# Gated DeltaNet's inverse: the third series of a join writes to the PSUM bank of the scan's state products

## The chip, the cores and the metric

The kernel runs on one core of one Trainium2 chip. The time is the device time of one execution in microseconds, from the chip's own clock. The profile is one execution taken with the hardware profiler. The engines are TensorE (PE in the profile; PEld is its loading of weights), VectorE (DVE), ScalarE (ACT), GpSimd (POOL) and SyncE (SP), whose queue issues most of the DMAs.

## The reference

Four layers of a decoder trunk on one sequence of 1024 positions, width 1024, all in float32: HGRN2, sliding-window attention, Gated DeltaNet, and HGRN2 again. Each layer normalises x, applies its mixer to it, gates the result and adds it back to x. The layer that the change touches is the third. Cut to its core, for one chunk of 64 positions of one of 16 heads:

```python
A = jnp.einsum('bhid,bhjd->bhij', kb, k_) * dec * strict
rhs = jnp.concatenate([v_ * beta_[..., None], kb * jnp.exp(d)[..., None]], axis=-1)
X = lax.linalg.triangular_solve(A + eye, rhs, left_side=True, lower=True, unit_diagonal=True)
u, w = X[..., :dv], X[..., dv:]
v_new = u - jnp.einsum('bhid,bhde->bhie', w, S)
o = jnp.einsum('bhid,bhde->bhie', q_ * jnp.exp(d)[..., None], S) + jnp.einsum('bhij,bhje->bhie', qk, v_new)
S = S * jnp.exp(d_last)[..., None] + jnp.einsum('bhid,bhie->bhde', k_ * jnp.exp(d_last - d)[..., None], v_new)
```

q, k and v come from an input projection, a causal convolution of four taps and a SiLU; q and k are normalised to unit length. The output is normalised, multiplied by a gate path z (SiLU) and projected back.

## The kernel before, in words

The kernel works with chunks of 128 positions. It forms the inverse of the triangular matrix (A plus the identity) outright and then multiplies with it. Two of the 16 heads share one q and k, so the layer runs in eight units (u = 0 to 7) of two heads. Three streams of work belong to a unit:

- The projections (proj_kq, proj_v, proj_z). One projection in proj_fm is 24 matmuls (eight blocks of the width, three products each, since the operands are split into a high and a low part) into one PSUM bank, for one half of the 1024 positions. Its evacuation follows: for q, k and v the convolution (conv: two copies on ScalarE, L692 and L696, three steps on VectorE, L698, a tanh, L704, and a last product, L705), then a transpose on TensorE (L711) and sums of squares on ScalarE (sumsq, L718); for z a tanh and a product (L789, L790). When both halves of q and k are through, the factors of the norms follow (L752 to L764), gd_gn among them.
- The inverse. kk_ps and qk_ps (L809, L810) are the products of k with k and with q for one half; they are evacuated with the decay and with gd_gn (L820, L824). The diagonal blocks of 32 by 32 go through DRAM into another layout and are inverted there by a forward substitution of 31 steps on VectorE (L845, L846, in gd_Tb). Then the blocks are joined to 128 by 128 in four series of small matmuls, for 16 matrices at once (two heads, eight chunks). The first (L874) and the second (L882 to L884) join 32 to 64 and write two tiles each, the third (L891) and the fourth (L899) join 64 to 128 and write one each. ScalarE and VectorE copy the results out between them: L885 copies the second series' result into gd_Z, which the third reads; L886 and L887 copy other parts of it into gd_uq; L895 and L896 copy the third's result into gd_Z for the fourth; L901 and L902 store the fourth's.
- The scan (scan). It goes through eight chunks in order with the state S: ks_ps (L942, L943), w_ps (L953, L969) and, in seven chunks of eight, S_ps (L958), which VectorE adds to the decayed state (L962, L964).

weave calls the streams in turn, by their shares of the work done so far, and so sets the order in which the code's instructions are written: first inverse(0) with projections of units 0 to 2, then scan(u) with inverse(u+1), projections and the adaLN product of the next layer. A scheduler at build time then orders each engine's queue: among the instructions that can go, those with the higher priority first, and otherwise those that were written first. The inverse's series have the highest priority (burst); tied keeps each series together.

PSUM has eight banks, handed out under tags by psum: "proj" has two, "lev" two (kk_ps, qk_ps and the tiles z_ps of the series), "ta", "tr", "o" and "s" one each. A tile holds its bank until its last reader is done. S_ps uses "ta". So do the projections in part: proj_ps counts its calls modulo self.pb and gives one call of pb = 3 to "ta". pb is 3 in most of the kernel, 2 in the weaves that have a scan of Gated DeltaNet (then no projection takes "ta"), and still 3 in the first weave:

```python
self.np_ = (self.np_ + 1) % self.pb
return self.psum("ta" if self.np_ == 2 else "proj", name, 1 if self.np_ == 2 else 2)
```

Buffers in SBUF have tags of the same kind; conv, sumsq and z's evacuation share "tb" with four.

Of the kernel before, what the change touches and what calls it, by code (L numbers as in the profile page):

```python
# [81 lines left out]
class Trunk:  # L82
# [501 lines left out]
    def gdn(self, i, side):  # L584
# [210 lines left out]
        def inverse(u, dd):  # L795
# [46 lines left out]
            for j in range(31):  # L842
                n, m = 31 - j, j // 2 + 1
# [22 lines left out]
            bank = lambda name, m: self.psum("lev", name, 2).rearrange("p (g m) -> p g m", m=m)  # L866
# [20 lines left out]
            nc.vector.tensor_copy(uv[R[0], :, R[1]], za[R[0]])  # L887
            yield 1300

            z = bank("z_ps", 64)  # L890
            self.tied([lambda g=g, q=q: nc.tensor.matmul(z[q, g % 8, :], uv[lo, g, up], Z[lo, g, :], start=True, stop=True)  # L891
                       for n in range(8) for g, q in ((n, up), (n + 8, lo))])
            for b in (0, 1):
# [4 lines left out]
            z = bank("z_ps", 64)  # L898
# [29 lines left out]
        def scan(u, dd):  # L928
# [3 lines left out]
            for n in range(C):  # L932
# [53 lines left out]
        decays()  # L986
        drain(proj_kq(0, ds[0], ((1,),)))
        weave(self.tc, (inverse(0, ds[0]), 28000, 0, 0.8, 100),
              (chain(proj_z(0, ds[0], (1,)), proj_v(0, ds[0]), proj_z(1, ds[1], (1,)), proj_kq(1, ds[1])), 62400, 0, 1, 0))
        self.pb = 2  # L990
        for u in range(U):
            cs = [proj_z(x, ds[x], hv) for x, *hv in ZL[u]]
            tot = 10400 * sum(len(z) - 1 for z in ZL[u])
            if u + 2 < U:
                cs.append(proj_kq(u + 2, ds[u + 2]))
                tot += 20800
            if u + 1 < U:
                cs.append(proj_v(u + 1, ds[u + 1]))
                tot += 20800
            st_ = [(scan(u, ds[u]), 18000, 0, 1, PR[0])]  # L1000
            if u + 1 < U:
                st_.append((inverse(u + 1, ds[u + 1]), 28000, 0, 1, PR[1]))
            else:
                self.fill_x(0)
                cs += [self.out_load(od, 0, KT, 0, gp, "tmp", 2, (self.zd, "tb", bufs["tb"])), self.out_mm(i, w_out, 0, KT, 0, on), self.out_load(od, 0, KT, 1, gp, "tmp", 2, (self.zd, "tb", bufs["tb"]))]
                tot += 41600
            weave(self.tc, *st_, (chain(*cs), tot, 0, 1, 0), (take(side, NS[2]), NS[2], 0, 1, 0))
# [644 lines left out]
```

## Time and profile before

| | |
|---|---|
| median of 3 runs | 2649.19 us (2645.78 to 2649.27) |
| profiled execution | 2648.82 us, span 2647.1 us |
| busy: TensorE, VectorE, ScalarE, GpSimd | 97%, 76%, 50%, 6% of the span |
| granted TensorE clock, mean over the span | 0.992 |
| Gated DeltaNet's inverses | the third series' first matmul at 1242.7 us, its last at 1859.8 us |
| DMA | 308.91 MB, 117 GB/s |

Times in the profile count from the span's start. A row of the timeline gives start, length, engine, line, operation and tiles, and in brackets how long the engine stood idle before it and what released it. A row of the windows gives, for each engine in turn, the busy time and the number of instructions, then the granted TensorE clock, the DMA share and GB/s. In a line's own view the pairs behind "its engine sat idle before it" are us in total and times.

### The profile page before, as it was taken

To read this page: it belongs to the slowest core of one execution; us is meant where nothing else is said; L and a number is where in the kernel's file an instruction comes from. 1 tells how busy PE (TensorE), PEld (TensorE's weight loads), DVE (VectorE), ACT (ScalarE), POOL (GpSimd) and SP (SyncE) were. 2 spreads that over 40 slices of the span, in tenths; PEclk is the share of its full clock that TensorE was granted. 3 is DMA by queue.
4 is the path that set the end of the run, shared out by engine and by line. 5 is a ranking of instruction groups with operands and counts; after the bars stand their busy time and mean duration, and the time that the engine had idled before them with its cause. 6 is when DMAs were issued, how large, how long until landed. Compare 5 with 4: busy or idle time off the path is not lost.

```text
span 2647.1 us, 50764 instructions
## 1 busy us (share of the span) xinstructions
PE 2560.9 (97%) x18271; PEld 2041.4 (77%) x18271; DVE 2016.7 (76%) x5651; ACT 1322.4 (50%) x3466; POOL 161.4 (6%) x382
## 2 busy tenths in 40 slices
PE   7999999999999999999999999999899999999998
PEld 4777777688878867777777777778678877787777
DVE  5485788777787878768899989988776837368675
ACT  3343444443464655545666666666544434245452
POOL 0001000011000000101000100110221000000010
PEclk8999999999999999999999999999999999999999
DMA  7333343544233252534444344333585312122343
GB/s 260 95 114 97 108 142 115 166 138 132 67 101 101 73 165 90 149 94 117 105 110 108 102 119 112 93 88 101 175 247 171 116 49 80 40 82 65 123 140 116
DMA packets 387281, 308.91 MB, mean 117 GB/s; under 512 B 74787, under 2 KB 313814, under 8 KB 387030
## 3 DMA queue, kind: packets, MB, share of 16 engines
q1 hardware_dynamic: 374486, 264.77, 34.4%
q0 software_dynamic: 12544, 40.90, 4.9%
q8 instruction: 144, 2.36, 0.4%
q14 instruction: 107, 0.88, 0.1%
HBM read 244.70 MB, written 60.88 MB: 115 GB/s over the span
## 4 chain that ended last, share of the span: by engine, by line
PE 74%; DVE 12%; DMA 5%; ACT 4%; issue 3%; SPq 0%; POOL 0%; DVEq 0%; POOLq 0%; ACTq 0%
PE proj_ps L222 10%; PE proj_ps L224 10%; PE proj_ps L223 10%; PE outp_ps L222 5%; PE outp_ps L223 5%; PE outp_ps L224 4%; PE projw_ps L223 2%; PE projw_ps L222 2%; PE projw_ps L224 2%; DVE gd_tb L698 1%; PE projt_ps L223 1%; PE projt_ps L224 1%; PE projt_ps L222 1%; DVE w_lo L194 1%; PE w_ps L953 1%
## 5 line engine op out<-in xcount | busy, mean ns | idle before, releaser
L222 PE MATMUL proj_ps<-hhi,w_hi 128*128 128x512 f32 x1664 | 676.7, 407 | 3.6 <-ACT gd_tb L696 3.3
L223 PE MATMUL proj_ps<-hlo,w_hi 128*128 128x512 f32 x1664 | 672.7, 404 | 0.0
L224 PE MATMUL proj_ps<-hhi,w_lo 128*128 128x512 f32 x1664 | 672.1, 404 | 0.0
L222 PEld LDWEIGHTS proj_ps<-hhi,w_hi 128*128 128x128 f32 x1664 | 315.0, 189 | 64.6 <-ACT gd_tb L696 5.9
L224 PEld LDWEIGHTS proj_ps<-hhi,w_lo 128*128 128x128 f32 x1664 | 314.7, 189 | 58.1 <-issue 0.4
L223 PEld LDWEIGHTS proj_ps<-hlo,w_hi 128*128 128x128 f32 x1664 | 315.2, 189 | 55.2 <-issue 0.9
L194 DVE TENSOR_TENSOR w_lo<-w_raw,w_hi 128x512 fp32r<-128x512 f32 x344 | 231.4, 677 | 142.3 <-ACT w_hi L193 139.6
L193 ACT CAST w_hi<-w_raw 128x512 fp32r<-128x512 f32 x344 | 209.5, 612 | 260.6 <-PE proj_ps L223 151.3
L222 PE MATMUL outp_ps<-o_hi,w_hi 128*128 128x512 f32 x576 | 230.2, 402 | 9.2 <-ACT o_hi L1323 7.4
L223 PE MATMUL outp_ps<-o_lo,w_hi 128*128 128x512 f32 x576 | 230.3, 400 | 2.4 <-DVE o_lo L1324 2.3
L224 PE MATMUL outp_ps<-o_hi,w_lo 128*128 128x512 f32 x576 | 228.8, 398 | 0.5 <-DVE w_lo L194 0.5
L196 ACT ACTIVATE w_hi<-w_raw,par 128x512 fp32r<-128x512 f32 (+1 forms) x136 | 94.8, 697 | 131.2 <-PE outp_ps L223 93.1
L698 DVE SCALAR_TENSOR_TENSOR gd_tb<-gd_xs,taps,gd_tb 128x512 f32<-128x512 f32 x192 | 146.2, 762 | 15.9 <-ACT gd_tb L696 12.0
L222 PEld LDWEIGHTS outp_ps<-o_hi,w_hi 128*128 128x128 f32 x576 | 109.5, 190 | 33.4 <-ACT o_hi L1323 9.1
L448 DVE SCALAR_TENSOR_TENSOR ada_acc<-ada_w,par,ada_acc 128x512 f32<-128x512 f32 x154 | 115.1, 748 | 21.1 <-DMA ada_w<-in_ada_w_dram 19.9
L223 PEld LDWEIGHTS outp_ps<-o_lo,w_hi 128*128 128x128 f32 x576 | 109.7, 190 | 26.3 <-DVE o_lo L1324 4.4
L197 DVE SCALAR_TENSOR_TENSOR w_lo<-w_raw,par,w_hi 128x512 fp32r<-128x512 f32 (+1 forms) x136 | 97.0, 716 | 41.4 <-ACT w_hi L196 40.7
L224 PEld LDWEIGHTS outp_ps<-o_hi,w_lo 128*128 128x128 f32 x576 | 109.5, 190 | 22.9 <-DVE w_lo L194 1.0
L1315 POOL DMA_DIRECT2D o_in<-od x72 | 38.8, 539 | 1214.9 <-DMA w_raw<-in_hg_out_w_dram 429.2
L222 PE MATMUL projw_ps<-w_hi,hhi 128*128 128x512 f32 x256 | 102.4, 405 | 2.3 <-DVE hg_q L1041 2.3
L223 PE MATMUL projw_ps<-w_lo,hhi 128*128 128x512 f32 x256 | 103.6, 406 | 0.2 <-DVE w_lo L194 0.2
L224 PE MATMUL projw_ps<-w_hi,hlo 128*128 128x512 f32 x256 | 102.2, 400 | 0.0
(429 smaller groups left out, 5365.7 us busy)
## 6 DMA issues: line engine op xcount, KB each, us to landing
ada_w<-in_ada_w_dram SPq DMA_DIRECT2D x160, 256.0 KB, 2.8
w_raw<-in_hg_in_w_dram SPq DMA_DIRECT2D x136, 256.0 KB, 2.8
w_raw<-in_gd_in_w_dram SPq DMA_DIRECT2D x128, 256.0 KB, 3.0
o_in<-od POOLq DMA_DIRECT2D x72, 256.0 KB, 3.5
x<-xd SPq DMA_DIRECT2D x64, 256.0 KB, 4.5
w_raw<-in_gd_out_w_dram SPq DMA_DIRECT2D x64, 256.0 KB, 3.2
xd<-x POOLq DMA_DIRECT2D x48, 256.0 KB, 2.7
w_raw<-in_sw_in_w_dram SPq DMA_DIRECT2D x44, 256.0 KB, 3.0
```

The lines of the kernel that those rows point to most:

```text
L193: nc.scalar.copy(hi, raw)
L194: nc.vector.tensor_tensor(lo, raw, hi.bitcast(F32), ALU.subtract)
L196: nc.scalar.activation(hi, raw, AF.Copy, scale=scale)
L197: nc.vector.scalar_tensor_tensor(lo, raw, scale, hi.bitcast(F32), ALU.mult, ALU.subtract)
L222: mm(out, a[0], b[0], start=start, stop=False)
L223: mm(out, a[0], b[1], start=False, stop=False)
L224: mm(out, a[1], b[0], start=False, stop=stop)
L448: self.step = self.nc.vector.scalar_tensor_tensor(acc, w, c, acc, ALU.mult, ALU.add)
L698: last = nc.vector.scalar_tensor_tensor(y, xs[:, j:j + HT], w(j), y, ALU.mult, ALU.add)
L953: nc.tensor.matmul(po[:, hd[a]], dd["u"][a, hf][:, cs], rhs, start=True, stop=True)
L1315: nc.gpsimd.dma_start(t, od[(k0 + k) * P:(k0 + k + 1) * P, sl])
```

## The change

One line of inverse is changed: the third series' tile is allocated under "ta", the tag of S_ps, and not under "lev". Shape, matmuls, priority and the copies behind it stay as they are. The fourth series' tile and all others stay in "lev".

```diff
             nc.vector.tensor_copy(uv[R[0], :, R[1]], za[R[0]])
             yield 1300
 
-            z = bank("z_ps", 64)
+            z = self.psum("ta", "z_ps", 1).rearrange("p (g m) -> p g m", m=64)
             self.tied([lambda g=g, q=q: nc.tensor.matmul(z[q, g % 8, :], uv[lo, g, up], Z[lo, g, :], start=True, stop=True)
                        for n in range(8) for g, q in ((n, up), (n + 8, lo))])
             for b in (0, 1):
                 nc.gpsimd.tensor_copy(uv[R[b], :, R[b]], Uc[R[b]])
             nc.scalar.copy(Z[up, 0:8], z[up])
             nc.vector.tensor_copy(Z[up, 8:16], z[lo])
```

## The prediction

> **What bounds the kernel now.** I read the page first, then the busy time by window over the Gated DeltaNet layer, then the third series' own line, then the timelines round it. The page gives the span and who fills it:
>
> ```profile
> span 2647.1 us, 50764 instructions
> PE 2560.9 (97%) x18271; PEld 2041.4 (77%) x18271; DVE 2016.7 (76%) x5651; ACT 1322.4 (50%) x3466; POOL 161.4 (6%) x382
> ...
> PE 74%; DVE 12%; DMA 5%; ACT 4%; issue 3%; SPq 0%; POOL 0%; DVEq 0%; POOLq 0%; ACTq 0%
> ```
>
> The chain of waits that ends last is 74% TensorE. The windows (length, then busy time per engine, PE first) show it for the stretch that the change touches:
>
> ```profile
> 1215.00:1250.00 35.00, 32.13 (x356) 25.96 (x357) 28.70 (x64) 21.23 (x67) 6.73 (x12) 1.00 0.48 123
> 1250.00:1870.00 620.00, 606.28 (x4415) 485.90 (x4414) 558.92 (x1625) 392.33 (x1244) 54.33 (x137) 0.99 0.41 107
> ```
>
> From 1250 to 1870 TensorE rests for 13.7 of 620 us, so a hole closed on TensorE should mostly be time, and a hole opened costs about its length. The third series is L891; its own view says what PE waited for:
>
> ```profile
> L891 PE MATMUL z_ps<-gd_Z,gd_uq x256: 218/218/312, 1242.7 to 1859.9; 64*64 64x64 f32 x128
> ...
>   DVE gd_uq L886: 7.2, 7
> ```
>
> Seven of its eight runs wait, 7.2 us in all, for VectorE's copy L886. L886 writes partitions 64 to 95 of gd_uq; the series reads partitions 0 to 63. It is no operand. L886 is the last reader of the second tile of the series before, so the wait is for that tile's bank in the ring of two. That is what the change removes.
>
> **The gain.** What then still holds the series is its operand gd_Z, copied by ScalarE at L885. The timelines of units 0, 4 and 7 (start, length in us; idle time and releaser in brackets):
>
> ```profile
> 1240.66 0.40 PE L222 MATMUL proj_ps<-hhi,w_hi 128*128 128x512 f32 x1
> 1241.64 0.58 ACT L885 COPY gd_Z<-z_ps 32x512 f32<-32x512 f32 x1
> 1242.66 1.15 PE L891 MATMUL z_ps<-gd_Z,gd_uq 64*64 64x64 f32 x32 [1.60 <-DVE gd_uq L886]
> ...
> 1600.85 0.58 ACT L885 COPY gd_Z<-z_ps 32x512 f32<-32x512 f32 x1 [0.33 <-PE z_ps L884]
> 1602.29 0.69 DVE L886 COPY gd_uq<-z_ps 32x512 f32<-32x512 f32 x1
> 1603.12 1.15 PE L891 MATMUL z_ps<-gd_Z,gd_uq 64*64 64x64 f32 x32 [1.03 <-DVE gd_uq L886]
> ...
> 1857.35 0.58 ACT L885 COPY gd_Z<-z_ps 32x512 f32<-32x512 f32 x1 [0.54 <-PE z_ps L884]
> 1858.97 1.15 PE L891 MATMUL z_ps<-gd_Z,gd_uq 64*64 64x64 f32 x32 [0.40 <-DVE gd_uq L886]
> ```
>
> In units 4 and 7 ScalarE is through (1601.43, 1857.93) before PE runs out of projection (1603.12 - 1.03 = 1602.09, 1858.57), and the whole hole goes. In unit 0 ScalarE ends at 1242.22, and some 0.3 of the 1.6 us could go. Units 1 to 7 hold 7.2 - 1.6 = 5.6 us. The matmuls and the two copies of the result (L895, L896) are the same in any bank. A wait can come back behind the hole, as VectorE keeps its queue: the fourth series of unit 0 stands 0.47 us for L896. So 5.6 is the most, 0 the least, and I take 85%: **-4.7 us**.
>
> **The new bank.** It is tag "ta", one buffer. In units 1 to 7 only the scan's S_ps (L958) uses it. In the code's order the series of unit u+1 stands after all seven S_ps of scan u and before those of scan u+1, which need this inverse's result:
>
> ```profile
> L958 PE MATMUL S_ps<-gd_ws,gd_kt x112: 377/379/483, 1250.4 to 1929.6; 128*128 128x256 f32 x112
> ```
>
> Unit 0's first S_ps starts at 1250.4, 4.2 us behind the series' last reader (L896, below, until 1246.16). No wait there: 0. In "lev" the fourth series and the next unit's kk_ps now find a bank earlier, but both wait for more than that (L896; the fourth series): 0 too.
>
> In the first weave it is otherwise. There proj_ps counts modulo three, and every third projection takes "ta". Counted through the code, 198 calls have been made when inverse(0) allocates the third series' tile; calls 199 and 200 follow, and 200 = 3*66 + 2 is the one that takes "ta". It is q of unit 1, second half. **In the code's order it stands behind the series; in time it ran long before it:**
>
> ```profile
> 1222.09 0.57 ACT L692 COPY gd_xs<-proj_ps 128x512 f32<-128x512 f32 x1
> 1228.37 0.58 ACT L692 COPY gd_xs<-proj_ps 128x512 f32<-128x512 f32 x1
> 1231.01 0.28 ACT L718 ACTIVATE gd_tb<-qtr_ps 128x128 f32<-128x128 f32 x1 [1.47 <-PE qtr_ps L711]
> 1232.03 0.71 ACT L696 ACTIVATE gd_tb<-proj_ps,taps 128x512 f32<-128x512 f32 x1
> 1238.17 0.93 DVE L705 SCALAR_TENSOR_TENSOR gd_q<-gd_tb 128x512 f32<-128x512 f32 x1
> 1243.24 0.28 ACT L718 ACTIVATE gd_tb<-qtr_ps 128x128 f32<-128x128 f32 x1
> 1245.01 0.60 ACT L789 ACTIVATE gd_tb<-proj_ps 128x512 f32<-128x512 f32 x1
> 1245.48 0.68 DVE L896 COPY gd_Z<-z_ps 64x512 f32<-64x512 f32 x1
> 1246.29 0.68 DVE L790 SCALAR_TENSOR_TENSOR gd_tb<-gd_tb,proj_ps 128x512 f32<-128x512 f32 x1
> 1248.53 0.48 PE L222 MATMUL proj_ps<-hhi,w_hi 128*128 128x512 f32 x1
> ```
>
> (The two L692, with L696, are the evacuations of q's halves; L718 their sums of squares; L789 and L790 evacuate the z projection behind them, and the last row starts the next one that then has a bank.) So it matters whether buffers of one tag are given out in the code's order or to whoever is ready. Two places speak for the code's order. The first is the ring of two:
>
> ```profile
> 1222.27 0.69 DVE L705 SCALAR_TENSOR_TENSOR gd_k<-gd_tb 128x512 f32<-128x512 f32 x1
> 1242.55 0.68 DVE L887 COPY gd_uq<-z_ps 32x512 f32<-32x512 f32 x1
> 1246.31 1.15 PE L899 MATMUL z_ps<-gd_uq,gd_Z 64*64 64x64 f32 x32 [0.47 <-DVE gd_Z L896]
> 1247.39 1.16 PE L809 MATMUL kk_ps<-gd_k 128*128 128x128 f32 x8
> ```
>
> After L887 (1243.23) one bank of "lev" is empty. Unit 1's kk_ps has had its k since 1222.96, yet starts only right behind the fourth series, which the code allocates first. The second is L789: the z projection's evacuation needs a buffer of tag "tb" and comes right behind the L718 of q's second half, whose buffer of that tag stands before it in the code. I take it that the order is the code's. Then call 200 waits for L896 of unit 0.
>
> **What that costs.** The projection leaves 1222 and starts behind L896. With its own VectorE work (L698, L705) and ScalarE work (L704, L696) gone from the inverse's way I put L896 some 3 us earlier, at 1243 (0 earlier is the other end). It is 24 matmuls; from the evacuation at 1222.09 to that at 1228.37 is 6.3 us with a transpose between, so 5.5 us alone, to 1248.5. Up to here TensorE has the z projections behind it (two banks "proj") to do in its stead, so nothing is lost yet. Then they are both full, and the next needs L790, which is queued behind the late one's evacuation. From evacuation to first L718 was 8.9 us for q's first half (1222.09 to 1231.01) and 14.9 for the second; I take 9, then L789 and L790, 1.3: the next projection starts at 1258.8 and not at 1248.5. In between TensorE has the scan; the projections' own share is:
>
> ```profile
> 1248.50:1258.00 9.50, 5.12 (x18) 3.09 (x18) 0.00 (x0) 0.00 (x0) 1.00 0.35 95
> 1278.00:1318.00 40.00, 15.42 (x62) 0.00 (x0) 1.00 0.27 73
> 1811.00:1842.00 31.00, 15.62 (x62) 0.00 (x0) 1.00 0.31 89
> 1252.85 0.17 DVE L762 TENSOR_SCALAR gd_gn<-gd_gm 128x16 f32<-128x16 f32 x1
> ```
>
> (first row: proj_ps alone; second and third: the forward substitution's gd_Tb in units 1 and 7.) 5.12/9.5 of 10.3 us is **+5.5 us**. The ends: 0, if other work fills the gap; 1246.2 + 5.5 + 14.9 + 1.3 = 1267.9, so 19.4 us late, times 0.54, +10.5.
>
> Third, the factor gd_gn, which the evacuation of unit 1's kk_ps needs, moves from 1252.9 to some 1263, and with it inverse(1). Its forward substitution is 15.4 us of VectorE work spread over 40 us, in unit 7 over 31, so some 9 of the 10 us can be caught up. I take **+1 us**, between 0 and +4.
>
> **The sum**, on the profiled execution's 2648.82 (span 2647.1 and 1.7 outside): -4.7 + 5.5 + 1.0 = +1.8, 2650.6. The median of the runs is 0.4 above that execution: **2651 us**. Its own range is 2645 (the whole 5.6 against a cost of 2) to 2659 (both upper ends).
>
> **Rivals.**
> One: buffers go to whoever is ready. Then call 200 has left "ta" (1232.7) ten us before the series, nothing stands against the gain, and the time is 2649.2 - 4.7 = 2644.5 (2643.6 with all 5.6). For it: L891 takes the bank that came free first, L886's, and not the one next in turn; that choice, though, is of a bank and not of who is served. Against it: the two places above.
> Two, on the slow side: lateness is not caught up. The scan of unit 1 needs inverse(1), and the k, q and v of later units need the buffers that this scan frees; if 10 us of lateness stand through the weave, the projections lack buffers at its end and TensorE rests for what is not absorbed. It decides from about 4 us on: -4.7 + 5.5 + 10 gives 2660, 2656 with 6. For it: TensorE's slack of 2% cannot make up anything itself. Against it: the substitution's spread, above.
> Three: the hole is hidden anyway, VectorE (559 of 620 us busy) ending what PE ended, and only the cost stays, or neither: 2649 to 2655.
>
> A stop of TensorE can also cost clock. At the start it stood 4.69 us, and the matmuls behind it were slow:
>
> ```profile
> 28.71 1.87 PE L432 MATMUL ada_row<-ada_w,par 128*1 128x512 f32 x2 [4.69 <-DMA ada_w<-in_ada_w_dram]
> L432 PE MATMUL ada_row<-ada_w,par x32: 590/592/1061, 14.1 to 46.5; 128*1 128x512 f32 x32
> ```
>
> The new gap is broken up by the scan's matmuls, so I add nothing; a stop of that length would belong to the second rival. The Trainium skill (TensorE: Matmul & The Clock Gate, Part 1: The HAM clock gate) has TensorE fall to half rate after an idle window of about 3.4 us and need about as long to come back; by that rule one unbroken stop in unit 0 would add an estimated 1.7 us to the sum, 2653. The 1061 ns beside 592 agrees.
>
> **How the numbers follow.** A difference under 0.2% (5.3 us) counts as none. The forecast gets 0.5: its range mostly lies within +-5.3, so 0.03 faster, 0.35 same, 0.12 slower. Rival one 0.15: 0.09 faster, 0.06 same, since 4.7 to 5.6 us is just at the bound. Rival two 0.2, all slower. Rival three 0.15: 0.01 faster, 0.14 same. Together 0.13, 0.55, 0.32. The range reaches from rival one's best (2643) to rival two's price (2661).
>
> **What would show it.** In the profile after: L891 no longer waits for L886, nor for anything in units 1 to 7, and PE's idle time there falls by some 5 us from 13.7. If the order is the code's, the L692 now at 1228.37 comes after unit 0's L896, near 1248, and L789 near 1257; if it stays before unit 0's series, the first rival holds. gd_gn near 1263, and the first series of unit 1 less than 3 us later than now, would show the lateness absorbed; 8 us or more later speaks for the second rival. The forecast is wrong if PE's idle time between 1248 and 1260 has not grown while the time rises, or if the waits at L891 remain.

## The result and the profile after

The change makes the kernel slower: 2661.51 us (median of 6 runs, 2660.34 to 2663.56) against 2647.68 (6 runs of the kernel before), a ratio of 1.0058 with a 95% interval of 1.0048 to 1.0069; the medians are 13.8 us apart. The forecast was 2651 in a range up to 2661. The profiled execution takes 2660.73 us, with 1.7 of it outside its span. Its page:

```profile
span 2659.0 us, 50745 instructions
PE 2571.9 (97%) x18271; PEld 2050.1 (77%) x18271; DVE 2014.7 (76%) x5651; ACT 1324.4 (50%) x3466; POOL 164.1 (6%) x382
```

The span grew by 11.9 us. TensorE's busy time for the same 18271 instructions grew by 11.0 (2560.9 before), its idle time by 0.9 (86.2 before, 87.1 after). So what was lost in the end is not rest of TensorE: it was slower at the same work. The mean granted clock is 0.988, before 0.992; the share not granted, times the span, is 31.9 us against 21.2, so 10.7 more (to some 2 us, as the clocks are given to three digits). The windows show where. Before (length, busy PE, PEld, DVE, ACT, POOL, granted clock, DMA share, GB/s):

```profile
1235.00:1250.00 15.00, 12.90 (x269) 10.48 (x268) 13.97 (x28) 10.01 (x28) 4.19 (x5) 1.00 0.52 146
1250.00:1260.00 10.00, 10.00 (x62) 8.79 (x61) 7.70 (x27) 4.15 (x14) 0.00 (x0) 1.00 0.26 64
1260.00:1280.00 20.00, 20.00 (x98) 15.64 (x96) 15.74 (x51) 13.47 (x45) 0.37 (x2) 1.00 0.62 163
```

After, the same stretches:

```profile
1235.00:1250.00 15.00, 9.77 (x239) 8.76 (x239) 8.35 (x12) 5.40 (x13) 4.35 (x6) 0.70 0.42 123
1250.00:1260.00 10.00, 8.84 (x47) 7.20 (x46) 3.10 (x5) 4.03 (x12) 0.00 (x0) 0.93 0.10 28
1260.00:1280.00 20.00, 16.55 (x61) 11.89 (x62) 13.79 (x47) 9.48 (x34) 0.00 (x0) 0.74 0.18 55
```

In these 45 us TensorE now rests for 9.8 us instead of 2.1, and the clock that it is not granted comes to 15 x 0.30 + 10 x 0.07 + 20 x 0.26 = 10.4 us, before 0. The timeline after, round unit 0's third series and behind it:

```profile
1241.08 0.25 PE L884 MATMUL z_ps<-gd_Z,gd_Uc 32*32 32x32 f32 x1 [2.01 <-issue]
1242.27 1.97 PE L891 MATMUL z_ps<-gd_Z,gd_uq 64*64 64x64 f32 x32 [0.82 <-ACT gd_Z L885]
1244.88 0.68 DVE L896 COPY gd_Z<-z_ps 64x512 f32<-64x512 f32 x1 [0.78 <-ACT gd_Z L895]
1245.71 1.97 PE L899 MATMUL z_ps<-gd_uq,gd_Z 64*64 64x64 f32 x32 [1.48 <-DVE gd_Z L896]
1251.70 0.37 ACT L954 ACTIVATE gd_ws<-w_ps,gd_gw 128x128 f32<-128x128 f32 x1 [1.18 <-PE w_ps L953]
1259.18 0.58 ACT L692 COPY gd_xs<-proj_ps 128x512 f32<-128x512 f32 x1
1259.66 0.69 ACT L696 ACTIVATE gd_tb<-proj_ps,taps 128x512 f32<-128x512 f32 x1
1260.40 0.70 PE L958 MATMUL S_ps<-gd_ws,gd_kt 128*128 128x256 f32 x2 [1.56 <-ACT gd_tb L696]
1270.77 0.58 ACT L789 ACTIVATE gd_tb<-proj_ps 128x512 f32<-128x512 f32 x1
1272.39 0.68 DVE L790 SCALAR_TENSOR_TENSOR gd_tb<-gd_tb,proj_ps 128x512 f32<-128x512 f32 x1
1273.13 0.50 PE L222 MATMUL proj_ps<-hhi,w_hi 128*128 128x512 f32 x1 [0.82 <-DVE gd_tb L790]
1276.20 0.17 DVE L762 TENSOR_SCALAR gd_gn<-gd_gm 128x16 f32<-128x16 f32 x1
```

The evacuation L692 of call 200 has gone from 1228.37 to 1259.18, behind unit 0's L896: the bank is handed out in the code's order. The wait of L891 for L886 is gone (0.82 for its own operand in its place), but the third and fourth series take 1.97 us each where they took 1.15, at half the clock. The next projection starts at 1273.13 (before 1248.53).

The scan is held back too. Its first S_ps (L958) ran at 1250.42 before:

```profile
1250.42 0.65 PE L958 MATMUL S_ps<-gd_ws,gd_kt 128*128 128x256 f32 x2
```

Now it starts at 1260.40, though its operand gd_ws is there from 1252.07 on (L954). TensorE is released by L696, which writes nothing that S_ps reads: it is the last reader of call 200's tile, and S_ps needs the same bank, "ta".

### The profile page after: what moved, and what is told of

The parts are those of the page before. It is cut to its first block, busy times and chain, and to the rows that moved or that the text cites. A ratio compares the mean times of both kernels' runs of the same rounds, so it can differ in the third digit from the quotient of the medians.

```text
span 2659.0 us, 50745 instructions
## 1 busy us (share of the span) xinstructions
PE 2571.9 (97%) x18271; PEld 2050.1 (77%) x18271; DVE 2014.7 (76%) x5651; ACT 1324.4 (50%) x3466; POOL 164.1 (6%) x382
## 4 chain that ended last, share of the span: by engine, by line
PE 74%; DVE 13%; ACT 5%; DMA 4%; issue 3%; SPq 1%; POOL 0%; DVEq 0%; ACTq 0%; POOLq 0%
PE proj_ps L222 10%; PE proj_ps L224 10%; PE proj_ps L223 10%; PE outp_ps L223 4%; PE outp_ps L222 4%; PE outp_ps L224 4%; PE projw_ps L223 2%; PE projw_ps L222 2%; PE projw_ps L224 2%; PE projt_ps L223 1%; PE projt_ps L222 1%; PE projt_ps L224 1%; DVE gd_tb L698 1%; DMA ada_w<-in_ada_w_dram 1%; DVE w_lo L194 1%
```

## The experiments

Each edit is made to the changed kernel where nothing else is said. The first four of them share 23 runs of the kernel before (median 2648.92), the last three 21 on another chip (median 2648.44).

**The bank in units 1 to 7 only.** Unit 0's third series stays in the ring, so call 200 has nothing to wait for.

```diff
-            z = self.psum("ta", "z_ps", 1).rearrange("p (g m) -> p g m", m=64)
+            z = bank("z_ps", 64) if u == 0 else self.psum("ta", "z_ps", 1).rearrange("p (g m) -> p g m", m=64)
```

> The third series in the scan's bank in units 1 to 7 only; unit 0 stays in the ring of two. Theory (the loss is call 200 of the projections, held back behind unit 0's series because buffers of one tag are given out in the code's order): the loss of unit 0 goes, the gain of units 1 to 7 stays, 2643 us against 2647.7 of before (2641 to 2645), L692 of that projection back near 1228 and no wait of L891 for L886 in units 1 to 7. Rival A (the move is bad in every unit, or any new order of the queues costs about 10 us): 2655 or more. Rival B (the gain is hidden, VectorE ends what PE ended): 2646 to 2649.

Measured: 2648.26 us (12 runs), ratio 0.9997 (0.9987 to 1.0007). The loss is gone, but the gain is not there either: -3.4 to +1.9 us by the interval. The time is the one that rival B gave.

**The bank in unit 0 only.**

```diff
-            z = self.psum("ta", "z_ps", 1).rearrange("p (g m) -> p g m", m=64)
+            z = bank("z_ps", 64) if u else self.psum("ta", "z_ps", 1).rearrange("p (g m) -> p g m", m=64)
```

> The third series in the scan's bank in unit 0 only. Theory: the whole loss without the gain, 2647.7 + 18 = 2666 (2663 to 2668), unit 1's first series near 1351. Rival A (a loss in every unit): about 2650. If it is 2661 like the changed kernel, units 1 to 7 give no gain.

Measured: 2666.55 us (4 runs), ratio 1.0063 (1.0046 to 1.0079). The whole loss comes from this one of eight units. The median is 5 us above that of the changed kernel, which by the expectation would be the gain of units 1 to 7; but the two ratios, 1.0063 and 1.0058, lie within each other's intervals, so this decides nothing. Its windows show the rest and the lower clock at the same places:

```profile
1235.00:1250.00 15.00, 9.02 (x236) 8.41 (x233) 7.66 (x10) 5.45 (x14) 3.55 (x5) 0.66 0.37 103
1260.00:1280.00 20.00, 17.00 (x56) 12.71 (x54) 12.73 (x46) 8.63 (x32) 0.00 (x0) 0.66 0.17 53
```

**The bank in all units, another projection in "ta".** The count modulo three is moved on by two before the first weave. The calls that take "ta" are then 189, 192, 195 and 198, and none of them stands behind unit 0's third series in the code while it could run before it.

```diff
         drain(proj_kq(0, ds[0], ((1,),)))
+        self.np_ += 2
         weave(self.tc, (inverse(0, ds[0]), 28000, 0, 0.8, 100),
```

> All eight third series in the scan's bank as in the changed kernel, and the count of proj_ps moved on by two before the first weave, so that calls 189, 192, 195 and 198 take that bank and not 191, 194, 197 and 200: none that takes it stands behind unit 0's series. Theory: as with units 1 to 7 alone, 2643 (2641 to 2646). Rival (the bank itself, or the series in unit 0, is what costs): 2655 or more.

Measured: 2649.74 us (10 runs), ratio 1.0009 (0.9995 to 1.0023). So the series may use this bank in every unit without a loss like that of the change; what costs is that call 200 has to share it in that order. Again no gain: the time lies between what the theory and what the rival gave.

**The lateness without the move.** The kernel before, all banks as they were; only the matmuls of call 200 are issued behind the last matmul of unit 0's fourth series. (tied is made to return its last matmul, and self.gd is set during the first weave alone; these lines are left out here.)

```diff
...
+            hold = self.gd and self.np_ == 2 and c0 == P
             for k in range(KT):
                 a = [x[:, k % 4, :] for x in w[k // 4]]
-                self.mm3(ps, a, (self.hhi[hf][:, k, :], self.hlo[hf][:, k, :]), k == 0, k == KT - 1)
+                with self.tc.issue_after(self.after4.ins) if hold else nullcontext():
+                    self.mm3(ps, a, (self.hhi[hf][:, k, :], self.hlo[hf][:, k, :]), k == 0, k == KT - 1)
...
-            self.tied([lambda g=g, q=q: nc.tensor.matmul(z[q, g % 8, :], Z[up, g, :], uv[up, g, up], start=True, stop=True)
+            self.after4 = self.tied([lambda g=g, q=q: nc.tensor.matmul(z[q, g % 8, :], Z[up, g, :], uv[up, g, up], start=True, stop=True)
```

> The kernel before, with every series in the ring of two, but with call 200 (q of unit 1, second half) issued on TensorE behind the last matmul of unit 0's fourth series. No bank is changed. Theory (it is the lateness of this one projection that costs): the same loss as in unit 0 of the changed kernel without its gain, 2666 (2662 to 2669), clock near 0.5 to 0.7 round 1245 and 1268. Rival (something else about the bank, such as the scan's S_ps waiting): 2648 to 2653.

Measured: 2662.96 us (4 runs), ratio 1.0053 (1.0038 to 1.0068): the loss of the change without the move of the series. Its windows show about the same rest and lost clock:

```profile
1235.00:1250.00 15.00, 9.49 (x210) 8.72 (x205) 7.11 (x10) 5.76 (x14) 3.79 (x5) 0.61 0.32 94
1260.00:1280.00 20.00, 16.93 (x73) 12.72 (x74) 13.85 (x47) 9.76 (x35) 0.00 (x0) 0.83 0.21 58
```

It does not tell the lateness of call 200 from the wait for its bank, the rival that the expectation named. Call 200 takes "ta" in the kernel before as well, and here the first S_ps (L962 in this kernel) waits for call 200's evacuation (L700) just as in the changed kernel:

```profile
PE S_ps L962 <- ACT gd_tb L700: 1.6, 1, 1.6
```

A late call 200 in a bank that the scan does not use was not tried.

**The z projections behind call 200 freed of it.** Their evacuation takes its buffer under another tag than "tb", so it needn't wait for the sums of squares of call 200, and two further projections find a bank.

```diff
-                    th = tl("tb")
+                    th = tl("of" if (u, list(halves)) == (2, [1]) else "tb")
```

> The changed kernel, with the two z projections of unit 2 that run in the late one's stead evacuated into tag of, not tb, so that their evacuation need not wait for the late projection's. TensorE then has two more projections (11 us) to do before the gap. Two parts of the loss are told apart: TensorE out of work (banks full, clock down) and inverse(1) late. If the first is most of it: 2650 (2646 to 2654), with unit 1's series still late by 10 us or more and that absorbed later. If the lateness of inverse(1) is what costs: 2659 or more.

Measured: 2657.76 us (8 runs), ratio 1.0035 (1.0023 to 1.0047): about a third of the loss (13.8 - 9.3 = 4.5 us) comes back. TensorE is kept busy again (2.1 us of rest in the 45, as before the change), yet a part of the clock is still lost, 3.4 us in these rows:

```profile
1235.00:1250.00 15.00, 12.98 (x223) 10.24 (x222) 8.34 (x12) 6.68 (x16) 4.15 (x6) 0.84 0.56 166
1250.00:1260.00 10.00, 10.00 (x83) 8.49 (x82) 4.36 (x7) 3.88 (x11) 0.00 (x0) 0.90 0.31 80
```

The time falls between the two that were expected, nearer to the one for a late inverse(1). That is still late here: the first series of unit 1 starts at 1347.3, before at 1331.6; and the first S_ps still starts at 1263.4, before at 1250.4.

**Another bank without a sharer.** All eight third series write to "s", which no projection uses.

```diff
-            z = self.psum("ta", "z_ps", 1).rearrange("p (g m) -> p g m", m=64)
+            z = self.psum("s", "z_ps", 1).rearrange("p (g m) -> p g m", m=64)
```

> All eight third series in the bank of ks_ps (tag s), which no projection uses. Theory: no projection is held back, 2643 (2641 to 2645), unit 0's wait shorter too, by 0.3 us. Rival (a new bank costs by itself): 2650 or more.

Measured: 2650.58 us (12 runs), ratio 1.0010 (0.9999 to 1.0021). The number is at the bound of the rival (2650 or more), but no loss is measured (-0.3 to +5.6 us by the interval), and for the third time no gain. What PE waited for in the series from 1247 to 1885 us (us in total, times, longest) suggests why; the kernel before:

```profile
PE z_ps L891 <- DVE gd_uq L886: 5.6, 6, 1.2
```

The third series in bank "s":

```profile
PE z_ps L899 <- DVE gd_Z L896: 3.1, 4, 1.1
PE z_ps L884 <- issue: 2.4, 3, 1.6
PE z_ps L891 <- ACT gd_Z L885: 1.1, 2, 0.8
```

The 5.6 us at the third series have become 6.6 at others: at the fourth series (L899) for VectorE's second copy of the third's result, in the middle of the second series, and at the third for its own operand. The kernel with the moved count has the same pattern (3.6 us at L899). The one with the bank in units 1 to 7 has not: 0.2 us at L899, 3.4 at L891, and 4.1 instead of 1.8 at a transpose of the projections (L711). Over units 1 to 7 (1250 to 1870) TensorE's rest is what it was, 13.7 us before, 13.2, 13.9 and 14.5 in the rows of units 1 to 7 only, of the moved count and of bank "s" (one row each):

```profile
1250.00:1870.00 620.00, 606.83 (x4453) 488.58 (x4450) 560.38 (x1632) 394.48 (x1247) 55.45 (x137) 0.99 0.41 107
```
```profile
1250.00:1870.00 620.00, 606.13 (x4413) 484.90 (x4411) 557.30 (x1626) 394.65 (x1246) 55.09 (x137) 0.99 0.41 107
```
```profile
1250.00:1870.00 620.00, 605.49 (x4411) 484.66 (x4412) 558.24 (x1625) 393.19 (x1243) 55.22 (x137) 1.00 0.41 107
```

**Keeping TensorE warm.** Twelve matmuls whose result nobody reads are added to unit 0, three behind each of the first two series and six behind the third, to hold the clock.

```diff
...
+            if u == 0:
+                wp = self.psum("s", "warm_ps", 1)
+                self.warm(wp, last, 3)
...
+            if u == 0:
+                self.warm(wp, last, 3)
...
+            if u == 0:
+                self.warm(wp, last, 6)
```

> The changed kernel with 12 added matmuls of 128x512 in unit 0's join (3, 3 and 6 behind the first, second and third series), whose results nobody reads; they keep TensorE busy for 2.8 us more where it stood. Nothing is left out. If the fallen clock lengthens the stretch from 1240 to 1254: the granted clock there near 1.00, not 0.5 to 0.8, call 200 through 3 to 5 us earlier, 2657 (2655 to 2659). If the clock costs nothing, or 12 matmuls do not hold it: 2661 to 2663.

Measured: 2668.85 us (6 runs), ratio 1.0075 (1.0057 to 1.0092). That is above everything that was expected. It did not hold the clock: the mean is 0.79 from 1240 to 1256 and again from 1256 to 1280, and the added work came on top (5.3 us in the rows below; the median is some 7 above that of the changed kernel). The timeline shows where the attempt broke:

```profile
1242.08 0.96 PE L162 MATMUL warm_ps<-hhi 128*128 128x512 f32 x3
1246.60 0.26 PE L893 MATMUL z_ps<-gd_Uc,gd_Z 32*32 32x32 f32 x1 [2.43 <-issue]
1246.96 1.65 PE L162 MATMUL warm_ps<-hhi 128*128 128x512 f32 x3
1250.44 2.68 PE L162 MATMUL warm_ps<-hhi 128*128 128x512 f32 x6
1253.05 1.15 PE L913 MATMUL z_ps<-gd_uq,gd_Z 64*64 64x64 f32 x32
```

Three of the added matmuls take 0.96 us before the stop of 2.43 us inside the second series and 1.65 behind it. The fourth series is at full clock again (1.15), but the second gap, behind call 200, is not filled by them. So this run doesn't say what a held clock would have been worth; it stays open.

The runs side by side. Rest and lost clock are from each profiled execution, summed over the three windows from 1235 to 1280 us; "against before" is the difference of the medians:

```
kernel                         against before   PE at rest   clock not granted
before                                             2.1 us        0.0 us
changed                          +13.8 us          9.8          10.4
bank in unit 0 only              +17.6            10.5          11.9
lateness, old banks              +14.0            10.1          10.3
z freed of call 200               +9.3             2.1           3.4
changed, 12 matmuls added        +20.4             7.1           8.6
bank in units 1 to 7 only         -0.7             1.7           1.7
count moved, all units            +0.8             1.7           0.0
bank "s", all units               +2.1             1.8           0.0
```

Every kernel in which call 200 is late has lost clock there, and only those lose time beyond the 5.3 us that count as none. The z row shows that the two columns don't add up to the time: of its 9.3 us they explain about 3.4. Over its 8 runs the lost clock of the whole span is 3.5 us higher than before (standard error 1.7) and the rest of the time 5.6 us (1.1). Where those 5.6 arise wasn't found; the late scan and the late inverse(1) are what this kernel still shares with the changed one.

## Why the prediction was wrong

**The bank's order: right.** "I take it that the order is the code's. Then call 200 waits for L896 of unit 0" held, as did the count that picked call 200: L692 is late, and moving the count or the bank takes the loss away. The first rival, buffers for whoever is ready, is out.

**"No wait there: 0" for the scan: wrong in unit 0.** For units 1 to 7 it held. In unit 0 the prediction looked only at the series as a neighbour of S_ps in "ta" (last reader 4.2 us earlier). But the late call 200 now lies in that bank between them. S_ps, in the code behind both, starts 10.0 us later and has stood with its operand ready for 8.3 of them (1252.07 to 1260.40). So "In between TensorE has the scan" was wrong as well: TensorE ran no matmul of the scan between L969 at 1253.41 and S_ps at 1260.40. What this wait alone costs in time no run shows.

**"So I add nothing" for the clock: this step failed.** It was argued that the scan's matmuls break up the gap, and only an unbroken stop was priced. Before call 200 it was unit 0's series that ran without projections between them; behind it the scan had only just been let go. PE's longest stop between 1235 and 1280 is the 2.01 us in the second series. The clock fell all the same, as windows of the kernel after show that are cut where it changes:

```profile
1237.02:1241.14 4.12, 1.19 (x92) 1.11 (x95) 3.20 (x4) 2.38 (x6) 2.46 (x4) 1.00 0.56 154
1241.14:1251.38 10.24, 7.94 (x86) 7.36 (x87) 3.50 (x5) 3.38 (x8) 0.00 (x0) 0.50 0.21 60
1251.38:1258.84 7.46, 7.46 (x43) 6.01 (x41) 2.41 (x4) 2.50 (x9) 0.00 (x0) 1.00 0.08 21
1258.84:1261.62 2.78, 0.70 (x3) 0.30 (x2) 1.86 (x5) 1.51 (x3) 0.00 (x0) 1.00 0.32 88
1261.62:1271.86 10.24, 8.53 (x23) 5.64 (x23) 4.92 (x13) 4.87 (x20) 0.00 (x0) 0.50 0.14 39
1271.86:1280.00 8.14, 7.32 (x37) 5.96 (x38) 7.70 (x32) 4.27 (x13) 0.00 (x0) 1.00 0.21 70
```

After 4.1 us with PE busy for 29%, and again after 2.8 us with 25%, the clock is at half for 10.2 us. It comes back only behind some 5 us of nearly unbroken work (from 1245.7 and from 1266.8). That is the term that should have stood at about +10 and stood at 0: the 10.7 us of clock over the whole span agree with the 11.0 of busy time. Over all runs (span times one minus the granted clock) it is 32.4 us in the 6 of the changed kernel and 22.4 in 44 of the kernel before, +10.0 with a standard error of 0.9; the rest of the time, span times clock, differs by +2.9 with one of 1.0. With only that rest the forecast's +1.8 would have been near, but by luck, since its terms did not hold one by one (below). The Trainium skill's rule that the prediction weighed (TensorE: Matmul & The Clock Gate, Part 1: The HAM clock gate), an idle window of about 3.4 us, was read there as one unbroken stop; the same page of the Trainium skill (A second HAM failure mode: psum-queue depth-cycling) also tells of a kernel whose short idles between groups of matmuls made the clock swing. The rows above agree with the second: no stop here is over 2.01 us.

**The hole on TensorE: +5.5 was too small, within its bound of 10.5.** It measured 9.8 - 2.1 = 7.7 us. One sentence of its working was wrong: "Up to here TensorE has the z projections behind it (two banks "proj") to do in its stead, so nothing is lost yet". They did run in its stead, at 1222 to 1236, and so were used up when the four series came. Before, 18 projection matmuls lay between unit 0's series, from 1236.6 to 1245.9; after, none. What PE waited for from 1235 to 1280 in the kernel after:

```profile
PE z_ps L884 <- issue: 2.0, 1, 2.0
PE S_ps L958 <- ACT gd_tb L696: 1.6, 1, 1.6
PE z_ps L899 <- DVE gd_Z L896: 1.5, 1, 1.5
PE z_ps L882 <- DVE gd_Z L876: 0.9, 1, 0.9
```

The waits at L884, L899 and L882 lie inside the series and had been covered (0.5 at L899 alone before); 5.2 of the 9.8 us are before 1250. The wait at L958 is the one for call 200's bank. L896 came 0.6 us earlier, not 3. And call 200 itself took from 1249.77 to 1258.84, 9.1 us and not 5.5, among kk_ps, qk_ps and the scan at a low clock, so the next projection starts 14.3 us behind the 1258.8 forecast. Over the whole span only 0.9 of the 7.7 are left, since TensorE rests less elsewhere: 1.6 us less ahead of 1235 and 5 less behind 1280 (for one, 593.61 of 605 us busy from 1280 to 1885, against 576.28 of 590 from 1280 to 1870 before, 2.3 us less):

```profile
1280.00:1885.00 605.00, 593.61 (x4347) 474.64 (x4346) 547.26 (x1592) 385.85 (x1215) 57.49 (x137) 1.00 0.41 109
```

**The gain of 4.7: not there.** The step "I take 85%" failed, though its warning stood beside it: "a wait can come back behind the hole". The waits of bank "s" above show it: L891 no longer waits for L886, and L899 waits for L896 instead. In units 5 and 6, which hold 2.2 of those 3.1 us, L896 ends 5.2 and 5.9 us behind the second series' last matmul in both kernels, since VectorE still has other work and the copies ahead of it to do. Three kernels that make the move without the lateness have about the same rest on TensorE in units 1 to 7, and none is measurably faster. In the kernel with the bank in units 1 to 7 the time at full clock is 3.5 us lower (standard error 0.7) and the lost clock 3.2 higher (1.3), so there something may have been won and given back; the other two don't show it, and it stays open.

**The lateness of inverse(1): +1 in the prediction.** The first series of unit 1 is 19.6 us later, where under 3 was forecast and 8 was to speak for the second rival. Before, and then after:

```profile
L874 PE MATMUL z_ps<-gd_Tc,gd_uq x64: 191/191/212, 1331.6 to 1332.6; 32*32 32x32 f32 x64
```
```profile
L874 PE MATMUL z_ps<-gd_Tc,gd_uq x64: 191/191/212, 1351.2 to 1352.2; 32*32 32x32 f32 x64
```

The rival's price, 2656 to 2660, came nearest, but its mechanism, projections that lack buffers at the weave's end, did not show: TensorE rests less behind 1280 than before. At unit 7 the first series is still 14.8 us late. It is argued, not shown, that the lateness stood because TensorE, busy for 97%, had nothing to make up lost work with; that this and the clock are the whole cause isn't shown either, as the z row of the table leaves 5.6 us open.

## What to carry to other kernels

A buffer tag that two streams share orders them as the code does: before a tile is moved to another tag, list who else draws on it, which later one ran earlier until now, and who then waits for that one's bank. A hole in TensorE's work is priced with the clock it costs: look at the busy share of the few microseconds round it, not only at its longest stop. And a wait removed ahead of a chain of copies may come back at the chain's next step, as it did here at L899: follow it to the last copy.

## What was not expected of the hardware

Two stretches of 4.1 and 2.8 us with PE busy for 29% and 25%, and no stop over 2.01 us, each took the clock down to 0.50 for 10.2 us. In all nine traces the granted clock is either 1.00 or 0.50, and its stretches at half last 3.41 us or a multiple of it, but for the one that the end of the program cuts. When each trace is cut into such steps of 3.41 us, from 100 to 2600 us, TensorE was busy for 17% to 68% of the step ahead of every fall (55 falls), and no step under 48% at full clock went without one. Between 48% and 68% both occur.

In unit 0 of all kernels with call 200 late, the second series stopped in its middle for 2.0 to 2.8 us, after 77 to 89 of its 96 matmuls, with nothing that the profile shows to wait for ("issue"). A stop of 1.6 us like it is in unit 3 with the moved count and with bank "s", where call 200 is not late. The kernel before has none; in its unit 0 other matmuls stand between the first and the second series. Each time a transfer of instructions on DMA queue q8 ran just ahead (1238.75 to 1239.71 in the changed kernel), and the matmuls went on 1.3 to 1.7 us behind its end, in the changed kernel at 1241.08. That the stop waits for these instructions fits, but was not tried.
